# A GLA and RWKV-7 hybrid step on one core: GLA states kept in DRAM between the passes, 28 row buffers, no precedence on TensorE for a pair's products, and transfers that the planner expects later

## Chip, cores and metric

One Trainium2 chip, of which the kernel uses one core. The metric is device time in microseconds (us) of the whole program, one launch; lower is better. TensorE is called PE here, VectorE DVE, ScalarE ACT, GpSimd POOL, and SyncE, which issues the transfers, SP.

## The reference

One layer of a decoder step over a prompt of 1024 tokens and 8 sample tokens, all in float32. Two branches run on the same input: gated linear attention (GLA, 4 heads with a state of 128 x 256) and RWKV-7 (16 heads with a state of 64 x 64, handled as 8 pairs of heads). Both carry a state along the tokens:

```python
p = jnp.einsum('btd,dn->btn', x, w_in)                      # 1024 -> 9360 columns
# GLA:  S_t = diag(a_t) S_{t-1} + k_t^T v_t ;  o_t = q_t S_t
o_gla, S_gla = _gla_chunked(q, k, v, log_a, S_gla0)
# RWKV: S_t = S_{t-1} (diag(w_t) - kk_t^T (kk_t * a_t)) + v_t^T k_t ;  y_t = S_t r_t
y, S_rwkv = _rwkv7_scan(r, w, k, v, kk, a, S_rwkv0)
m = sigmoid(gate_a) * (o_gla @ w_up_gla) + sigmoid(gate_b) * (o_rwkv @ w_up_rwkv)
y_out = _layernorm(DEEPNORM_ALPHA * x + m @ w_out, ln_g, ln_b, LN_EPS)
```

The outputs are `y_out` of both groups and the new states.

## The kernel before

**Passes.** The prompt is cut into two passes: pass 0 has 512 prompt tokens and the 8 sample tokens (matmuls of 260 columns, two per weight block), pass 1 the other 512 (matmuls of 512 columns). Each pass projects all columns of `w_in`, block by block of 128. A weight block and the input are split into a high and a low part (`whi`, `wlo`, `xh`, `xl`), and each product is three matmuls, `proj<-xh,whi`, `proj<-xl,whi` and `proj<-xh,wlo`. Pass 0 writes the split weights to DRAM (`wh`, `wl`), pass 1 reads them back. After both passes come the up-projections of GLA and RWKV for both passes, which load their inputs from DRAM (`o_gla`, `o_rwkv`), and at the end the product with `w_out`.

**What runs beside the projection.** Each of the 8 pairs of a pass is a stream of operations (`pair`): `front` prepares factors and writes the masked products `gg<-big`; SP then copies four blocks of `gg` to DRAM (`LD<-gg`) and reads them back rearranged (`wide<-LD`); DVE solves triangular systems from that in 31 steps (`Xt<-X,wide`, `X<-X,Xt`); and `chain` carries the pair's state over 8 chunks of 64 tokens. One chunk of the chain is a loop through two engines: PE `pch<-wide,gg`, DVE copies it (`rh<-pch`), PE `pch<-rh,XT`, a copy to `wide`, PE `pch<-wide`, and DVE makes the next state (`wide<-pch,pc,s0p`), from which the next chunk starts. The chains of the 16 pairs (8 in each pass) run one after another. Each of the 4 GLA heads is another stream (`gla_head`), and so are the weight splits, the evacuations and the gates.

**What sets the order.** All streams are merged at build time by a planner (`Order.run`) that writes one fixed order for each engine and for SP's queue; on the chip each engine works through its own order, and an instruction whose input is late holds those behind it. The planner takes, of the operations that are next in their streams, the one with the smallest key: its expected start, less a precedence. For operations on PE the precedence is `ON_PE[kind]`, for other engines `PRIO[kind]`, both in us. The expected start adds `HOP[by]` to the time when an input is ready, `by` being the engine that made it, `D` for a transfer:

```python
key = t - (s.on_pe if s.op.eng == "P" else s.prio)
```

A stream names its kind as it goes on: `pair` in `front`, then `turn` (its transposes), `chain` and `norm`; GLA's heads are `head`, the projection `block` with a precedence of 0.

**Buffers.** `SBUF` lists the rotating buffers; `row` is the common one, 128 x 520 float32, of which there are 26. `GS` holds the four GLA states, 128 x 256 each, in SBUF: pass 0 leaves a head's state there and pass 1 starts from it.

Of the kernel before, what the change touches and what calls it, by code (L numbers as in the profile page):

```python
# [10 lines left out]
F32 = mybir.dt.float32  # L11
# [9 lines left out]
P = 128  # L21
D = 1024
# [4 lines left out]
HT = TP // 2  # L27

PASS = [(0, HT + NS, NS, [(0, 260), (260, 260)]), (HT + NS, HT, 0, [(0, 512)])]
GH, GDK, GDV = 4, 128, 256  # L30
# [5 lines left out]
NGC = HT // GC  # L36
# [7 lines left out]

HALF = HT + NS
SBUF = {
    "row": ([P, HALF], 26), "wide": ([P, 2 * HT], 4), "gg": ([P, 4 * HT], 2), "lw": ([P, HT], 2),
    "l2s": ([P, 2 * P], 1), "pc": ([P, NCH], 3), "X": ([P, 256], 1),
    "Xt": ([P, P], 1), "S": ([P, GDV], 2), "s0p": ([P, C], 2), "rh": ([P, P], 2),
    "sto": ([P, P], 1), "Xs": ([P, 3 * P], 1), "bnd": ([P, 1], 3), "st": ([P, 32], 3), "part": ([P, HALF], 2), "l2p": ([P, 2 * P], 2),  # L50
# [10 lines left out]
SPARE_ROWS = 8  # L61


HOP = {"P": 0.2, "D": 0.26, "G": 0.14, "V": 0.14, "A": 0.14}

SWITCH = 0.09
HOLD = 0.11
# [7 lines left out]

PRIO = {"evacuate": 0.7, "pair": 0.4, "turn": 0.5, "chain": 0.5, "norm": 0.1, "x": 0.7, "lora": 0.2, "rank": -0.3,
        "head": 0.3, "gate": 0.05, "w": 0.3, "out": -0.1, "state": 0, "block": 0.0}
ON_PE = {"evacuate": 0.0, "pair": 0.15, "turn": 0.1, "chain": 0.15, "norm": 0.15, "x": 0.0, "lora": 0.15, "rank": 0.1,
         "head": 0.1, "gate": 0.06, "w": 0.0, "out": -0.03, "state": 0.1, "block": 0.0}

URGENT = 0.6
# [62 lines left out]
def price(eng, name, out, args, ins):  # L144
# [3 lines left out]
    if eng == "P":  # L148
# [8 lines left out]
        return 2 * (m + n) / 1200 * rows * cols / P ** 2  # L157
    if eng == "S":
        return 0.48
# [45 lines left out]
class Engine:  # L205
# [3 lines left out]
    def __getattr__(self, name):  # L209
        def make(out, *args, **kw):  # L210
# [3 lines left out]
            for eng, handle in self._handles.items():  # L214
                call = getattr(handle, "tensor_copy" if (eng, name) == ("V", "copy") else name)
                ways.append((eng, lambda call=call: call(out, *args, **kw), price(eng, name, out, args, ins)))  # L216
                if eng in "VG" and shared(eng, name, out, ins):
                    port += eng
            if eng == "S":
                lag = transfer(out, args[0])  # L220
# [8 lines left out]
class Stream:  # L229
# [4 lines left out]
    def be(self, name):  # L234
        self.kind, self.prio, self.on_pe = name, PRIO[name], ON_PE[name]


class Order:
# [4 lines left out]
    def __init__(self, nc):  # L243
        self.P, self.A, self.V, self.G, self.S, self.E, self.C = (Engine(**e) for e in (
            {"P": nc.tensor}, {"A": nc.scalar}, {"V": nc.vector}, {"G": nc.gpsimd}, {"S": nc.sync},
            {"V": nc.vector, "G": nc.gpsimd}, {"A": nc.scalar, "V": nc.vector}))
# [75 lines left out]
    def start(self, op):  # L322

        best = None
        for eng, fn, cost in op.ways:
            free, t = self.time[eng] + (SWITCH if eng == "P" and op.tiles != self.tiles else 0.0), 0.0
            for x in (op.out, *op.ins):
                at, by = self.ready.get(x.tensor.name, (0.0, None))
                if eng == "S" and by == "D" and x is op.out:
                    continue  # L330
                if by != eng:
                    at += HOP.get(by, 0.0) + (SPARE if eng == "P" and by in ("V", "A", "G") else 0.0)
                elif eng != "P" and x is not op.out:
# [70 lines left out]
class Kern(Order):  # L404
# [71 lines left out]
    def setup(self):  # L476
        nc, a = self.nc, self.a
        E = mybir.EngineType
        self.es.enter_context(self.tc.manual_schedule(engines={E.PE, E.Activation, E.DVE, E.Pool, E.SP}))
        cp = self.pool("const")  # L480
        wp = self.pool("w", side="left")
        self.dr = self.pool("dr", space=DRAM)
        pp = self.pool("psum", space=PSUM)
        xp = self.pool("x", side="right")
        self.r1 = r1 = self.pool("work", side="left")
        for tag, bufs in BANKS.items():
            self.buffers(tag, bufs, lambda tag=tag, bufs=bufs: pp.tile([P, 512], F32, name=tag, bufs=bufs))
        for tag, (shape, bufs) in SBUF.items():
            dt = F32R if tag in PARTS else F32
            self.buffers(tag, bufs, lambda tag=tag, shape=shape, bufs=bufs, dt=dt:  # L490
                         r1.tile(shape, dt, name=tag, bufs=bufs))
        for tag, (shape, bufs) in WBUF.items():
            dt = F32 if tag == "wraw" else F32R
            self.buffers(tag, bufs, lambda tag=tag, shape=shape, bufs=bufs, dt=dt:
                         wp.tile(shape, dt, name=tag, bufs=bufs))
        for k in range(NK):
            for v in "hl":
                tag = f"x{v}{k}"
                self.buffers(tag, 1, lambda tag=tag: xp.tile([P, HALF], F32R, name=tag, bufs=1))
        nc.scalar.preload_act_table_set(EXP)  # L500
        self.cons = cp.tile([P, CST_W], F32, name="cons")
        self.pv = cp.tile([P, PV_W], F32, name="pv")
        self.ident = self.cst("ident")
        self.omu = cp.tile([P, NRC], F32, name="omu")
        self.oka = cp.tile([P, 8], F32, name="oka")
        self.nkk = cp.tile([P, 8], F32, name="nkk")
        self.bias = {}
        for n, v in [("glaeps", GLA_EPS), ("gneps", GN_EPS), ("lneps", LN_EPS), ("one", 1.0),
                     ("kkl", 0.5 * math.log(KK_SCALE))]:
            t = cp.tile([P, 1], F32, name="b_" + n)  # L510
            nc.vector.memset(t, v)
            self.bias[n] = t
        dbg = getattr(self, "dbg", {})
        self.o_gla = dbg.get("o_gla", None) or self.dr.tile([D, T], F32, name="o_gla")
        self.o_rwkv = dbg.get("o_rwkv", None) or self.dr.tile([D, T], F32, name="o_rwkv")
        self.sg = [[[self.dr.tile([P, PASS[i][1]], F32, name=f"sg{i}{n}{k}") for k in range(NK)] for n in range(2)]
                   for i in range(2)]
        self.mg = [[self.dr.tile([P, PASS[i][1]], F32, name=f"mg{i}{k}") for k in range(NK)] for i in range(2)]

        self.lev = cp.tile([P, 64 * MASKED], F32, name="lev")  # L520

        self.onesr = cp.tile([P, P], F32R, name="onesr")
        self.headsr = cp.tile([P, P], F32R, name="headsr")
        self.wa = cp.tile([P, NK * 16], F32, name="wa")
        self.alr = [cp.tile([96, HALF], F32R, name=f"alr{n}") for n in range(2)]
        self.gw2 = cp.tile([96, GH * GDK], F32R, name="gw2")
        self.GS = [cp.tile([P, GDV], F32, name=f"GS{h}") for h in range(GH)]

        self.smp = cp.tile([P, 4, NPAIR, NS], F32, name="smp")
        self.RS = self.dr.tile([4, NS, D], F32, name="RS")  # L530
        self.WA = self.dr.tile([2, NS, D], F32, name="WA")
        self.tail = cp.tile([P, NS + 1, NRC], F32, name="tail")
        self.carry = cp.tile([P, NRC], F32, name="carry")
        self.shT = cp.tile([P, NRC, NS], F32, name="shT")
        self.reset = cp.tile([P, HT], U8, name="reset")
        nc.vector.memset(self.reset, 1)
        nc.vector.memset(self.reset[:, ::C], 0)

        self.Sp = [cp.tile([P, C], F32, name=f"Sp{n}") for n in range(NPAIR)]
        for t in self.Sp:  # L540
            nc.gpsimd.memset(t, 0.0)

        for tag, n, bufs in (("az", 4 * HT, 2), ("XT", 2 * HT, 2), ("Lp", HT, 1), ("As", HT, 1)):
            ts = [cp.tile([P, n], F32, name=f"{tag}{i}") for i in range(bufs)]
            for t in ts:
                nc.gpsimd.memset(t, 0.0)
            self.fixed(tag, ts)
# [222 lines left out]
    def gla_head(self, c, h, rows, g):  # L770
        a, n, A, V, E, S_ = self.a, c.n, self.A, self.V, self.E, self.S
# [38 lines left out]
        for lv, m in enumerate(LEVELS):  # L810
            nb = P // (2 * m)
            pl = (yield from self.bank("big", [P, NGC, nb, m])) if lv else None
            wide = lv < MASKED
# [25 lines left out]
            self.free(*([pl] if lv else [r, r2, dd]))  # L839
            tot = nt_  # L840

        S = self.GS[h] if c.i else None

        def vk(x):
            s = slice(x * P, (x + 1) * P)
# [9 lines left out]
        for x in range(NGC):  # L855
            s = slice(x * P, (x + 1) * P)
            VKn = (yield from vk(x + 1)) if x < NGC - 1 else None
            pb = yield from self.bank("big", [P, 4, P])
            po, pS = pb[:, 0:2], pb[:, 2:4].rearrange("p a b -> p (a b)")
            for j in range(2):  # L860
                yield self.P.matmul(po[:, j], VK[:, j * P:(j + 1) * P], AT[:, x], start=True, stop=(S is None))
                if S is not None:
                    yield self.P.matmul(po[:, j], S[:, j * P:(j + 1) * P], qp_[:, s], start=False, stop=True)
            yield self.P.matmul(pS, VK[:, 2 * P:], VK[:, 0:GDV], start=True, stop=True)
            for j in range(2):
                yield A.copy(v[j][:, s], po[:, j])
            Sn = self.GS[h] if x == NGC - 1 else (yield from self.get("S"))
            if S is not None:
                yield V.scalar_tensor_tensor(Sn, S, tot[:, x:x + 1], pS, ALU.mult, ALU.add)
                if x:  # L870
                    self.free(S)
            else:
                yield V.tensor_copy(Sn, pS)
            self.free(pb)
            S, VK = Sn, VKn
        if c.i:
            yield S_.dma_start(self.o["gla_p"][0, 0, h], S)
        else:
            yield from self.gla_sample(h, q, k, v, al, [(AT_, z), (km_, vk1)], qp_)
        s0, s1 = z, vk1  # L880
        self.free(AT_, q, k, al)
# [806 lines left out]
```

## Time and profile before

| | us |
|---|---|
| median of 3 runs | 1630.18 (1628.06 to 1632.21) |
| the profiled execution, its own time | 1629.18 |
| its span, first to last instruction | 1627.4 |
| PE busy | 1579.8 (97%) |
| weight loads of PE (PEld) busy | 1394.6 (86%) |
| DVE busy | 1226.9 (75%) |
| ACT busy | 844.6 (52%) |
| POOL busy | 92.3 (6%) |

Shares are of the span. A matmul's end is modelled, and neighbouring matmuls overlap in the record, so a wait on PE shows only where it is longer than that overlap. The granted TensorE clock was 0.992 over the span. Line numbers say little here, since a helper in line 216 (`make` in `Engine`) records nearly every operation: the names of the tiles tell which is which.

### The profile page before, as it was taken

How to read it: one execution, taken by the hardware profiler on the slowest of the kernel's cores; microseconds unless marked ns; L12 is line 12 of the kernel's file. 1: busy time of each engine (PE TensorE's matmuls, PEld its weight loads, DVE VectorE, ACT ScalarE, POOL GpSimd, SP SyncE). 2: the span in 40 equal slices, each digit the busy share in tenths (PEclk: the TensorE clock that was granted, in tenths of full speed). 3: DMA queues.
4: the chain of work that ended last, by engine and by line, in shares of the span. 5: the costliest groups of instructions: out<-in, count | busy, mean ns of one | idle time of the engine just before them, and what ended most of it. 6: DMA issues, size and time to landing. Idle time of an engine off the chain costs nothing.

```text
span 1627.4 us, 29876 instructions
## 1 busy us (share of the span) xinstructions
PE 1579.8 (97%) x10066; PEld 1394.6 (86%) x10066; DVE 1226.9 (75%) x3201; ACT 844.6 (52%) x2054; POOL 92.3 (6%) x185
## 2 busy tenths in 40 slices
PE   8999999999999999999999999999999999999998
PEld 7899999989999998788877887788788889977786
DVE  6786897788888887678677987898676784666555
ACT  5446765656566656463625472446354555554210
POOL 1100000101010000000100011100000000000000
PEclk9999999999999999999999999999999999999999
DMA  9877785696568765754465546544654487789432
GB/s 291 254 228 235 219 263 174 188 285 207 168 199 284 220 205 173 235 166 131 149 187 156 149 148 208 178 115 150 188 156 132 139 251 226 253 276 289 155 111 84
DMA packets 339572, 318.42 MB, mean 196 GB/s; under 512 B 103011, under 2 KB 225004, under 8 KB 339420
## 3 DMA queue, kind: packets, MB, share of 16 engines
q1 hardware_dynamic: 339420, 316.52, 62.9%
q8 instruction: 80, 1.31, 0.4%
q14 instruction: 72, 0.59, 0.1%
HBM read 197.55 MB, written 117.82 MB: 194 GB/s over the span
## 4 chain that ended last, share of the span: by engine, by line
PE 71%; DVE 12%; DMA 6%; SPq 4%; ACT 3%; issue 2%; POOL 0%; POOLq 0%; DVEq 0%; ACTq 0%
PE proj L216 41%; PE big L216 20%; PE pY L216 6%; SPq L216 4%; PE pch L216 4%; DVE row L216 4%; DVE X L216 2%; DVE wide L216 2%; DVE Xt L216 1%; DMA wide<-LD 1%; ACT row L216 1%; DMA wlo<-wl 1%; DVE wlo L216 1%; DMA row<-xT 1%; DMA row<-o_gla 1%
## 5 line engine op out<-in xcount | busy, mean ns | idle before, releaser
L216 PE MATMUL proj<-xh,whi 128*128 128x260 f32 (+1 forms) x1872 | 617.3, 330 | 3.8 <-DMA whi<-wh 3.1
L216 PE MATMUL proj<-xh,wlo 128*128 128x260 f32 (+1 forms) x1872 | 617.0, 330 | 1.5 <-DMA wlo<-wl 1.0
L216 PE MATMUL proj<-xl,whi 128*128 128x260 f32 (+1 forms) x1872 | 616.7, 329 | 0.0
L216 PEld LDWEIGHTS proj<-xh,whi 128*128 128x128 f32 x1872 | 355.5, 190 | 29.9 <-issue 4.6
L216 PEld LDWEIGHTS proj<-xh,wlo 128*128 128x128 f32 x1872 | 355.3, 190 | 28.7 <-issue 3.0
L216 PEld LDWEIGHTS proj<-xl,whi 128*128 128x128 f32 x1872 | 355.4, 190 | 23.3 <-issue 2.5
L216 ACT CAST whi<-wraw 128x512 fp32r<-128x512 f32 x210 | 130.0, 621 | 100.1 <-PE proj L216 51.5
L216 DVE TENSOR_TENSOR row<-row 128x512 f32<-128x512 f32 (+9 forms) x334 | 164.1, 498 | 11.7 <-ACT row L216 4.2
L216 DVE TENSOR_TENSOR wlo<-wraw,whi 128x512 fp32r<-128x512 f32 x205 | 141.3, 692 | 39.4 <-ACT whi L216 35.8
L216 ACT ACTIVATE row<-row 128x512 f32<-128x512 f32 (+4 forms) x229 | 138.1, 610 | 38.1 <-DVE row L216 28.7
L216 DVE TENSOR_TENSOR Xt<-X,wide 128x60 f32<-128x60 f32 (+24 forms) x496 | 105.1, 212 | 43.2 <-DMA wide<-LD 32.4
L216 ACT ACTIVATE row<-proj,omu 128x260 f32<-128x260 f32 (+1 forms) x99 | 54.3, 548 | 137.9 <-PE proj L216 137.2
L216 PE MATMUL big<-row 128*128 128x64 f32 (+4 forms) x712 | 115.9, 280 | 2.8 <-DVE row L216 1.8
L216 DVE TENSOR_TENSOR X<-X,Xt 128x60 f32<-128x60 f32 (+24 forms) x496 | 105.0, 212 | 12.5
L216 ACT ACTIVATE s0p<-wide,pc 64x64 f32<-64x64 f32 x256 | 87.9, 343 | 41.7 <-DVE wide L216 37.7
L216 PEld LDWEIGHTS big<-row 128*128 128x128 f32 (+1 forms) x712 | 98.1, 192 | 12.5 <-DVE row L216 4.6
L216 ACT COPY wide<-pch 64x64 f32<-64x64 f32 x216 | 44.6, 207 | 97.5 <-PE pch L216 94.2
L216 DVE SCALAR_TENSOR_TENSOR wide<-pch,pc,s0p 64x64 f32<-64x64 f32 x224 | 63.0, 281 | 42.7 <-PE pch L216 38.5
L216 DVE SCALAR_TENSOR_TENSOR row<-proj,pv,row 128x259 f32<-128x259 f32 (+1 forms) x99 | 56.4, 570 | 42.3 <-ACT tail L216 28.7
L216 ACT COPY row<-big 128x128 f32<-128x128 f32 (+7 forms) x161 | 46.0, 309 | 68.0 <-PE big L216 66.7
L216 POOL TENSOR_TENSOR row<-row 128x512 f32<-128x512 f32 (+5 forms) x35 | 38.2, 1092 | 580.7 <-ACT row L216 188.7
L216 PE MATMUL big<-az,wide 128*128 128x256 f32 x256 | 65.9, 382 | 0.3 <-ACT wide L216 0.2
(255 smaller groups left out, 2647.4 us busy)
## 6 DMA issues: line engine op xcount, KB each, us to landing
wraw<-w_in SPq DMA_DIRECT2D x146, 256.0 KB
wh<-whi SPq DMA_DIRECT2D x146, 256.0 KB
wl<-wlo SPq DMA_DIRECT2D x146, 256.0 KB
whi<-wh SPq DMA_DIRECT2D x146, 256.0 KB
wlo<-wl SPq DMA_DIRECT2D x146, 256.0 KB
wide<-LD SPq DMA_DIRECT2D x64, 128.0 KB
wraw<-w_up_gla SPq DMA_DIRECT2D x32, 256.0 KB
wraw<-w_up_rwkv SPq DMA_DIRECT2D x32, 256.0 KB
```

What stands on the lines that cost most here:

```text
L216: ways.append((eng, lambda call=call: call(out, *args, **kw), price(eng, name, out, args, ins)))
```

## The change

Four edits. (1) The GLA states `GS` become DRAM tensors: pass 0 writes a head's last state there, pass 1 reads it into an `S` buffer just ahead of its first use, and the last state always lies in an `S` buffer, of which there are still 2. (2) `row` has 28 buffers instead of 26. (3) `ON_PE` is 0.0 for `pair`, `turn`, `chain` and `norm` (0.15, 0.1, 0.15 and 0.15 before). (4) `HOP["D"]` is 0.8 instead of 0.26.

```diff
-    "row": ([P, HALF], 26), "wide": ([P, 2 * HT], 4), ...
+    "row": ([P, HALF], 28), "wide": ([P, 2 * HT], 4), ...
...
-HOP = {"P": 0.2, "D": 0.26, "G": 0.14, "V": 0.14, "A": 0.14}
+HOP = {"P": 0.2, "D": 0.8, "G": 0.14, "V": 0.14, "A": 0.14}
...
-ON_PE = {"evacuate": 0.0, "pair": 0.15, "turn": 0.1, "chain": 0.15, "norm": 0.15, "x": 0.0, "lora": 0.15, "rank": 0.1,
+ON_PE = {"evacuate": 0.0, "pair": 0.0, "turn": 0.0, "chain": 0.0, "norm": 0.0, "x": 0.0, "lora": 0.15, "rank": 0.1,
...
-        self.GS = [cp.tile([P, GDV], F32, name=f"GS{h}") for h in range(GH)]
+        self.GS = [self.dr.tile([P, GDV], F32, name=f"GS{h}") for h in range(GH)]
...
-        S = self.GS[h] if c.i else None
+        S = None
+        if c.i:
+            S = yield from self.get("S")
+            yield S_.dma_start(S, self.GS[h])
...
-            Sn = self.GS[h] if x == NGC - 1 else (yield from self.get("S"))
+            Sn = yield from self.get("S")
             if S is not None:
                 yield V.scalar_tensor_tensor(Sn, S, tot[:, x:x + 1], pS, ALU.mult, ALU.add)
-                if x:
-                    self.free(S)
+                self.free(S)
...
-        if c.i:
-            yield S_.dma_start(self.o["gla_p"][0, 0, h], S)
-        else:
+        yield S_.dma_start(self.o["gla_p"][0, 0, h] if c.i else self.GS[h], S)
+        self.free(S)
+        if not c.i:
             yield from self.gla_sample(h, q, k, v, al, [(AT_, z), (km_, vk1)], qp_)
```

The same matmuls are issued as before; what moves is their order, and that of the other engines. Three places show how.

DVE, fifth pair of pass 1: from the last masked product `gg` to the first step of the solve, `Xt<-X,wide`, which needs the transfer `wide<-LD`. Before:

```order
L216 TENSOR_TENSOR gg<-big,cons 128x512 x4
L216 TENSOR_REDUCE st<-row 128x8
L216 TENSOR_TENSOR row<-st,row 128x512
L216 TENSOR_TENSOR row<-row 128x512 x2
L216 COPY rh<-pch 128x128
L216 TENSOR_TENSOR row<-row 128x512 x2
L216 TENSOR_REDUCE row<-row 128x8
L216 SCALAR_TENSOR_TENSOR wide<-pch,pc,s0p 64x64 x2
L216 COPY rh<-pch 128x128
L216 TENSOR_TENSOR Xt<-X,wide 128x31
```

The same place now, from the first update of the chain's state on:

```order
L216 SCALAR_TENSOR_TENSOR wide<-pch,pc,s0p 64x64 x2
L216 TENSOR_TENSOR row<-st,row 128x512
L216 TENSOR_TENSOR row<-row 128x512
L216 COPY rh<-pch 128x128
L216 TENSOR_TENSOR row<-row 128x512 x2
L216 COPY wide<-pch 64x64 x2
L216 TENSOR_TENSOR row<-row 128x512
L216 SCALAR_TENSOR_TENSOR wide<-pch,pc,s0p 64x64 x2
L216 TENSOR_REDUCE row<-row 128x8
L216 SCALAR_TENSOR_TENSOR row<-row 128x512
L216 COPY rh<-pch 128x128
L216 TENSOR_TENSOR Xt<-X,wide 128x31
```

A second update of the chain's state, with the copies on both sides of it, has moved ahead of the solve's first step. Over all 16 pairs, 303 DVE instructions now stand between a pair's last `gg` and its first `Xt`, 208 before: more in 12 pairs, as many in 2, fewer in 2 (14 became 9, 10 became 7).

SP, seventh pair of pass 1: the trip through DRAM and the reload of split weights that follows. Before:

```order
L216 DMA LD_15300<-gg 32x8x32 x4
L216 DMA Lp_184<-gg 32x4x32 x4
L216 DMA wide<-LD_15300 32x1024 x4
L216 DMA whi<-wh_0_7966 128x512
L216 DMA wlo<-wl_0_7969 128x512
```

The same place now:

```order
L216 DMA LD_15298<-gg 32x8x32 x4
L216 DMA Lp_184<-gg 32x4x32 x4
L216 DMA whi<-wh_0_7884 128x512
L216 DMA wide<-LD_15298 32x1024 x4
L216 DMA wlo<-wl_0_7918 128x512
```

One weight load has moved between the write of `LD` and its read. Every pair now has some transfer besides `Lp` at that place; before, 5 of 16 had.

PE, fourth chunk of the sixth chain of pass 1: from the chunk's first product to the product that needs DVE's copy `rh`. Before:

```order
L216 MATMUL pch<-wide,gg 128x128
L216 MATMUL pY<-az_177,wide 128x128
L216 MATMUL proj<-xl_9744,whi 128x512
L216 MATMUL proj<-xh_9703,wlo 128x512
L216 MATMUL proj<-xh_9712,whi 128x512
L216 MATMUL pch<-rh,XT_181 128x128
```

The same place now:

```order
L216 MATMUL pch<-wide,gg 128x128
L216 MATMUL pY<-az_177,wide 128x128
L216 MATMUL proj<-xl_9621,whi 128x512
L216 MATMUL proj<-xh_9616,wlo 128x512
L216 MATMUL proj<-xh_9629,whi 128x512
L216 MATMUL proj<-xl_9691,whi 128x512
L216 MATMUL pch<-rh,XT_181 128x128
```

One more matmul of the projection stands between the two. Over the 128 chunks it is 7.5 matmuls on average there, 6.4 before, and 7.7 instead of 6.5 between `pch<-rh,XT` and `pch<-wide`.

More of the change, by code (lines that the diff above doesn't have):

```diff
@@ L46 @@
 SBUF = {
-    "row": ([P, HALF], 26), "wide": ([P, 2 * HT], 4), "gg": ([P, 4 * HT], 2), "lw": ([P, HT], 2),
+    "row": ([P, HALF], 28), "wide": ([P, 2 * HT], 4), "gg": ([P, 4 * HT], 2), "lw": ([P, HT], 2),
     "l2s": ([P, 2 * P], 1), "pc": ([P, NCH], 3), "X": ([P, 256], 1),
```

## The prediction

> **What bounds the kernel now.** I read the shares of busy time first, then the span in three stretches, then PE's waits, and then followed the two largest of them back through the timelines of DVE and SP.
>
> ```profile
> PE 1579.8 (97%) x10066; PEld 1394.6 (86%) x10066; DVE 1226.9 (75%) x3201; ACT 844.6 (52%) x2054; POOL 92.3 (6%) x185
> ```
> ```profile
> 0.00:40.00 40.00, 34.95 (x254) 29.11 (x255) 28.37 (x64) 21.45 (x49) 7.80 (x19) 1.00 0.93 292
> 40.00:1580.00 1540.00, 1505.23 (x9620) 1332.47 (x9620) 1173.25 (x3096) 821.20 (x1998) 81.70 (x163) 0.99 0.64 196
> 1580.00:1627.40 47.40, 39.65 (x195) 33.01 (x194) 25.24 (x42) 1.99 (x8) 2.77 (x3) 0.95 0.26 89
> ```
>
> The columns behind the stretch are the busy time of PE, PEld, DVE, ACT and POOL. PE bounds the kernel, and the change takes no matmul away, so only PE's idle time can be won: 1627.4 - 1579.8 = 47.6 us. Of it 5.0 us lie in the first 40 us and 7.8 us in the last 47, where nothing that the change touches runs; 34.8 us are left between. Who ends those waits is in the list of PE's waits (total, times, longest):
>
> ```profile
> PE big L216 <- DMA row<-xT: 7.1, 3, 4.0
> PE pch L216 <- DVE wide L216: 6.2, 7, 2.0
> PE pch L216 <- DVE rh L216: 4.5, 5, 1.5
> PE big L216 <- DVE part L216: 3.2, 7, 0.9
> PE proj L216 <- DMA whi<-wh: 3.1, 2, 2.5
> PE big L216 <- DVE row L216: 1.8, 3, 0.9
> ...
> PE proj L216 <- DMA wlo<-wl: 1.0, 1, 1.0
> ...
> PE big L216 <- DVE l2p L216: 0.6, 1, 0.6
> ...
> PE proj L216 <- ACT row L216: 0.4, 1, 0.4
> ```
>
> The chain of the pairs (`pch`) has the most, 10.7 us in 12 waits, always for DVE; transfers have 4.1 us at the projection's weights. DVE is only 75% busy, so why is it late? Its own largest wait for a transfer:
>
> ```profile
> DVE Xt L216 <- DMA wide<-LD: 32.4, 13, 4.6
> ...
> DVE l2p L216 <- DMA l2s<-lora: 13.2, 10, 5.8
> ```
>
> In 13 of 16 pairs DVE stands at the first step of the solve, 2.5 us on average, until the trip through DRAM has landed. What that does to PE is seen twice in the timelines, here in the fifth pair of pass 1, first DVE, then PE:
>
> ```profile
> 1049.08 0.29 DVE L216 COPY rh<-pch 128x128 f32<-128x128 f32 x1 [1.01 <-PE pch L216]
> 1052.53 0.19 DVE L216 TENSOR_TENSOR Xt<-X,wide 128x31 f32<-128x31 f32 x1 [3.16 <-DMA wide<-LD]
> ...
> 1054.04 0.59 DVE L216 SCALAR_TENSOR_TENSOR wide<-pch,pc,s0p 64x64 f32<-64x64 f32 x2
> ```
> ```profile
> 1052.36 0.38 PE L216 MATMUL pY<-gg,wide 128*128 128x128 f32 x2
> 1054.78 0.46 PE L216 MATMUL pch<-wide,gg 128*128 128x128 f32 x2 [2.04 <-DVE wide L216]
> ```
>
> The chain's update of `wide` stood in DVE's order behind `Xt`, which waited 3.16 us; PE paid 2.04 us of that. The other, in the sixth chain of pass 1, again DVE, then PE:
>
> ```profile
> 1208.40 0.19 DVE L216 TENSOR_TENSOR Xt<-X,wide 128x31 f32<-128x31 f32 x1 [2.27 <-DMA wide<-LD]
> 1208.62 0.29 DVE L216 COPY rh<-pch 128x128 f32<-128x128 f32 x1
> ```
> ```profile
> 1207.39 0.39 PE L216 MATMUL proj<-xh,wlo 128*128 128x512 f32 x1
> 1207.62 0.40 PE L216 MATMUL proj<-xh,whi 128*128 128x512 f32 x1
> 1208.97 0.49 PE L216 MATMUL pch<-rh,XT 128*128 128x128 f32 x2 [0.95 <-DVE rh L216]
> ```
>
> These rows also give a unit: matmuls of 512 columns start 0.23 us apart, while a record lasts 0.39, so that waits under about 0.16 us do not show as idle.
>
> **The planner's transfers expected later (`HOP`).** It puts more work ahead of whatever needs a transfer. From the order: 303 DVE instructions instead of 208 between a pair's last `gg` and its first `Xt`. At DVE's mean of 1226.9 / 3201 = 0.38 us the 95 more are 36 us, 2.3 us for a pair, against a mean wait of 2.5 us. That would fill the wait, were it spread evenly; it isn't: two pairs get fewer instructions and two as many as before. The sixth chain's wait above belongs to one of the latter, with 6 instructions before and now. I take 60% of the 32.4 us as filled. What PE gets of it: at most all of its 10.7 us of `pch` waits, at least nothing (PE's waits may have other causes, and the solve's later start moves the pair's later steps). PE pays 2.04 of 3.16 us in one example and 0.95 of 2.27 in the other, about half; over the 13 waits it can't have been as much, since 10.7 us are all there is. Half of the 10.7 us is my value: **-5.5 us**. The cover that DVE's fill uses is work that was due anyway; were it gone, the solve would wait again, and PE with it.
>
> The same edit puts a weight load between the write and the read of `LD` on SP, which before went out behind them:
>
> ```profile
> 1198.95 1.80 SPq L216 DMA_DIRECT2D LD<-gg  x4
> ...
> 1203.52 1.86 SPq L216 DMA_DIRECT2D wide<-LD  x4
> 1205.47 0.37 SPq L216 DMA_DIRECT2D whi<-wh  x1
> ```
>
> The read started 2.8 us after the four writes were issued (1198.95 + 1.80), and the `whi` load stood behind it. Now it fills that time. If its buffer is still held by PE, it delays the read instead; the row above that waits for `wide<-LD` would then grow. PE's waits for weights are 3.1 + 1.0 us, and one for `row<-xT` at the change of passes is what 7.1 leaves beside the start, about 2. Ends: -6.1 and, with one more wait as long as the longest, +2.5. I take **-2 us**.
>
> **No precedence for a pair's products (`ON_PE`).** With 0.15 the planner chose a pair's product over a projection matmul that could start up to 0.15 us sooner, so PE was planned to stand; with 0.0 it no longer is. From the order: one matmul more (7.5 for 6.4, 7.7 for 6.5) between a chain's products and the next that depends on them, 0.12 us in pass 0 (half the width) or 0.23 us in pass 1. A wait can lose no more than that. The list has some 25 waits for DVE's products that a pair's PE work shows; at 0.2 us each that is 5 us, beside waits too short to show. The other end is 0 on those rows, or a loss if the longer chain delays something. It can't be the end of the kernel. The last chain's products start at 1410.4:
>
> ```profile
> L216 PE MATMUL pch<-wide x256: 270/273/377, 147.5 to 1410.4; 128*128 128x128 f32 x128
> ```
> ```profile
> 1435.51 5.59 PE pY L216 x24
> ...
> 1608.47 5.55 PE pY L216 x24
> ```
>
> In the order the last chain ends 5844 projection matmuls into the program, 5891 before, and the blocks that need its result begin at 6216. From 1435 us to the end the chain of waits shows groups of 24 matmuls of 512 columns, the first and last of which stand here, in 5.6 us, 0.23 each: the tail streams. I take **-2.5 us**, half of the visible part.
>
> **GLA states through DRAM.** Eight transfers of 128 KB more, 4 writes in pass 0 and 4 reads in pass 1; no engine's work grows. A transfer of that size, issue on SP and first use on DVE:
>
> ```profile
> 1266.09 0.61 SPq L216 DMA_DIRECT2D l2s<-lora  x1
> ```
> ```profile
> 1269.45 0.29 DVE L216 CAST l2p<-l2s 128x256 fp32r<-128x256 f32 x1 [0.39 <-DMA l2s<-lora]
> ```
>
> 3.4 us. A write is waited for only by the same head's read, a pass later; on SP it stands until DVE's last state is made, as the store of the output did in pass 1, with `vd` and weight transfers behind it. Each read stands on SP behind weight loads that wait for a buffer; from the matmul that frees that buffer to the first that reads `S`, PE's order has 25, 35, 34 and 36 matmuls. The 25 are 12 of 512 columns at 0.23 and 13 of 128 columns in full float32 at about 0.22, 5.6 us, more than 3.4 + 0.6; the others have over 7 us. Ends: 0, and 4 x 3.4 = +13.6 us if PE stood for each read in full. I take **0**, since three reads have twice the time needed. [...]
>
> **28 rows.** PE's waits name the release of a bank by ACT's copy to `row` with 0.4 us. Ends -0.4 and 0; I take 0. The two rows enter the order above all.
>
> **The sum.** -5.5 - 2 - 2.5 + 0 + 0 = -10 us on the profiled execution's 1629.2 (span 1627.4 and 1.8 around it): 1619.2. It lies 1.0 below the median of the runs, 1630.2, so that I predict **1619.5**.
>
> **Rivals.** (a) The waits only move. 32.4 us of DVE's waits go, but the solve starts later, other products queue behind it, and PE finds new ones; the fewer instructions in two pairs speak for it, the 12 pairs with more against it. It gives 1629, give or take 5. Chance 0.18. (b) Slower: the reads of `S` are exposed. If SP is held past the point above, a read issued late is waited for by PE directly, in order, with `pb`'s bank held. It decides when SP is more than 5.6 - 4.0 = 1.6 us late for the tightest head and 3.5 for the rest. SP's queue is in fact held by PE and DVE often, which speaks for it; the planner's 0.8 for transfers speaks against. With half of the gains above kept it gives 1629 + 13.6 - 5 = 1638. Chance 0.12, with other losses of that size. (c) A much larger gain. The chain is freed altogether, all 10.7 us, and `part`, `row`, weights, in all 3.2 + 1.8 + 4.1 more, and hidden waits of 5 us: 1629 - 25 = 1604. Chance 0.08. [...]
>
> **How the numbers follow.** The forecast, a gain of 5 to 20 us, has 0.62. The measurement can't tell less than about 0.3%, 4.9 us, from no change. Faster: 0.62 + 0.08 = 0.70; same 0.18; slower 0.12. The range reaches from (c)'s edge, 1606, to 1633, which takes in (a) and leaves out most of (b) and half of (c): under 2 in 10.
>
> **What would show it.** DVE's row for `Xt` waiting for `wide<-LD` falls from 32.4 us to 10 to 20, in fewer pairs; PE's two `pch` rows from 10.7 to about 5; PE's idle time from 47.6 to 37 or 38. A row of PE waiting for `S<-GS` over 2 us makes the GLA term wrong; `whi` or `wlo` rows over 5 us the term of SP. The prediction is wrong if the row of `Xt` falls and the time doesn't.

## The result and the profile after

The changed kernel takes 1607.01 us (median of 4 runs, 1605.45 to 1607.85); the kernel before, run beside it, 1629.12 (4 runs, 1621.84 to 1632.21). The ratio is 0.987, with a 95% interval of 0.9835 to 0.9904. The profiled execution took 1607.75 us, 21.4 less than that of before. First the shares of busy time, then the span in three stretches (us; busy time of PE, PEld, DVE, ACT, POOL; granted clock, DMA share, GB/s):

```profile
PE 1568.2 (98%) x10066; PEld 1394.8 (87%) x10066; DVE 1225.4 (76%) x3206; ACT 835.5 (52%) x2046; POOL 91.7 (6%) x184
```
```profile
0.00:40.00 40.00, 34.33 (x250) 28.79 (x251) 28.57 (x64) 21.23 (x48) 7.80 (x19) 1.00 0.90 288
40.00:1559.00 1519.00, 1494.65 (x9628) 1333.29 (x9627) 1171.68 (x3102) 812.30 (x1990) 81.09 (x162) 0.99 0.65 200
1559.00:1606.00 47.00, 39.21 (x193) 32.68 (x191) 25.10 (x41) 1.99 (x8) 2.77 (x3) 0.96 0.27 90
```

The gain has two parts. PE's idle time fell from 47.6 to 1606.0 - 1568.2 = 37.8 us, all of it in the middle stretch (34.8 to 24.4). And PE's busy time fell by 11.6 us with the same 10066 matmuls. I read this as waits shorter than the overlap of two records, which a profile counts as busy (0.16 us between two matmuls of 512 columns, which start 0.23 us apart with records of 0.39); what supports that reading is measured further below. PE's waits (total, times, longest), and DVE's two rows for transfers:

```profile
PE big L216 <- DMA row<-xT: 5.7, 2, 4.0
PE big L216 <- DVE Sp L216: 5.5, 2, 2.9
PE pch L216 <- DVE wide L216: 2.7, 5, 1.1
PE pch L216 <- DVE rh L216: 2.3, 4, 1.0
PE big L216 <- ACT part L216: 2.1, 1, 2.1
PE big L216 <- DMA S<-GS: 1.7, 2, 1.0
...
PE proj L216 <- DMA wlo<-wl: 0.5, 1, 0.5
...
PE big L216 <- DVE part L216: 0.4, 1, 0.4
```
```profile
DVE Xt L216 <- DMA wide<-LD: 18.6, 10, 3.6
...
DVE l2p L216 <- DMA l2s<-lora: 4.2, 4, 1.4
```

The chain's two rows have halved (10.7 to 5.0), the weights' are nearly gone (4.1 to 0.5). One wait is new: 5.5 us for `Sp`, the state at a chain's end that PE transposes. It is the old mechanism at another place. First DVE, then PE, at 1135 us in pass 1:

```profile
1134.92 0.19 DVE L216 TENSOR_TENSOR Xt<-X,wide 128x31 f32<-128x31 f32 x1 [3.60 <-DMA wide<-LD]
...
1137.67 0.59 DVE L216 SCALAR_TENSOR_TENSOR Sp<-pch,pc,s0p 64x64 f32<-64x64 f32 x2
```
```profile
1138.32 0.42 PE L216 MATMUL big<-cons,Sp 128*64 128x128 f32 x1 [2.95 <-DVE Sp L216]
```

`Sp` stood in DVE's order behind the first four steps of the next pair's solve, eight instructions. The first of them stood 3.60 us for `LD`, and the eight then took 2.75 us; PE's wait of 2.95 us began 0.4 us after DVE's had ended. And PE paid once more. The same core in three stretches of 3.3 us: during the wait, just after it, and after that:

```profile
1134.70:1138.00 3.30, 0.67 (x3) 0.19 (x1) 2.74 (x10) 0.91 (x2) 1.26 (x1) 1.00 1.04 386
1138.30:1141.60 3.30, 3.29 (x9) 2.61 (x10) 2.70 (x11) 1.00 (x3) 0.00 (x0) 0.51 0.31 94
1141.80:1145.10 3.30, 3.30 (x15) 2.66 (x15) 2.85 (x14) 0.00 (x0) 0.00 (x0) 1.00 0.26 88
```

After the wait the granted clock was 0.51, and 9 matmuls started where 14 start at 1.00 (the counts in the rows take in those still running at a row's start), though PE reads as fully busy in both. Matmuls of 512 columns started 0.43 us apart in it and 0.23 us apart after it. Such a stretch at half clock costs about half its length, an estimate: 0.47 of it by this spacing, 0.49 by the clock, 0.36 by the counts. Before and after the change have four of them, 20.5 us in all in either, so that they don't explain the 11.6 us of busy time.

### The profile page after: what moved, and what is told of

Read it like the earlier page. It is cut to its first block, busy times and chain, and to the rows that moved or that the text cites. A ratio compares the mean times of both kernels' runs of the same rounds, so it can differ in the third digit from the quotient of the medians.

```text
span 1606.0 us, 29861 instructions
## 1 busy us (share of the span) xinstructions
PE 1568.2 (98%) x10066; PEld 1394.8 (87%) x10066; DVE 1225.4 (76%) x3206; ACT 835.5 (52%) x2046; POOL 91.7 (6%) x184
## 4 chain that ended last, share of the span: by engine, by line
PE 84%; DVE 6%; DMA 4%; ACT 2%; issue 2%; SPq 1%; POOL 0%; POOLq 0%; DVEq 0%; ACTq 0%
PE proj L216 49%; PE big L216 22%; PE pY L216 8%; PE pch L216 5%; DVE row L216 2%; SPq L216 1%; DMA wide<-LD 1%; DVE wide L216 1%; DVE Xt L216 1%; ACT row L216 1%; DVE X L216 1%; DMA wlo<-wl 1%; DMA S<-GS 1%; DVE az L216 0%; ACT wide L216 0%
## 5 line engine op out<-in xcount | busy, mean ns | idle before, releaser
L216 PEld LDWEIGHTS proj<-xh,whi 128*128 128x128 f32 x1880 | 356.5, 190 | 25.8 <-issue 1.7
L216 DVE TENSOR_TENSOR row<-row 128x256 f32<-128x256 f32 (+10 forms) x327 | 162.1, 499 | 16.4 <-ACT row L216 6.8
L216 ACT ACTIVATE row<-row 128x512 f32<-128x512 f32 (+5 forms) x229 | 138.4, 611 | 34.7 <-DVE row L216 24.2
L216 DVE TENSOR_TENSOR Xt<-X,wide 128x60 f32<-128x60 f32 (+24 forms) x496 | 108.3, 218 | 30.4 <-DMA wide<-LD 18.6
L216 DVE TENSOR_TENSOR X<-X,Xt 128x60 f32<-128x60 f32 (+24 forms) x496 | 105.0, 212 | 11.6
L216 PEld LDWEIGHTS big<-row 128*128 128x128 f32 (+1 forms) x712 | 94.2, 190 | 9.9 <-DVE row L216 2.3
L216 POOL TENSOR_TENSOR row<-row 128x512 f32<-128x512 f32 (+3 forms) x42 | 47.5, 1137 | 663.2 <-DVE row L216 223.7
```

## The experiments

Each ratio is to the kernel before, run beside it on the same chip, with its 95% interval. The experiments were measured in three groups, in which the median of before was 1624.2, 1622.8 and 1624.3 us (23, 17 and 11 runs). `HOLD`, a cost that the planner adds in another choice and that no part of the change touches, served to make neutral reorderings: the same work and settings, another order, and for a few operations another engine (DVE has 3188 instructions instead of 3201 in the first).

**Transfers expected later, alone** (on the kernel before):

```diff
-HOP = {"P": 0.2, "D": 0.26, ...
+HOP = {"P": 0.2, "D": 0.8, ...
```

> The kernel before with the planner's hop for transfers at 0.8 alone. Mechanism theory (the hop fills DVE's wait for the trip through DRAM): DVE's row of Xt waiting for wide<-LD falls from 32.4 us to under 22, PE's two pch rows from 10.7 to under 7, time 8 to 14 us under before. Precedence theory (the hidden short waits are the larger half, and they go with ON_PE): row of Xt falls all the same, time only 3 to 7 us under before. Reshuffling theory (any new order moves the time by some us, whichever edit makes it): no tie between the row of Xt and the time; anything from -12 to +8 us.

Measured: 1630.31 us, 1.0047 (1.0028 to 1.0066), slower by 0.5%: of the three ranges that were set for it only that of reshuffling holds it. PE's waits and DVE's row:

```profile
PE pch L216 <- DVE wide L216: 6.7, 7, 2.3
...
PE big L216 <- DVE Xs L216: 6.1, 2, 4.1
PE pch L216 <- DVE rh L216: 5.8, 10, 1.4
PE proj L216 <- DMA wlo<-wl: 3.0, 1, 3.0
```
```profile
DVE Xt L216 <- DMA wide<-LD: 19.5, 10, 4.8
```

DVE's wait for `LD` fell as in the whole change, from 32.4 to 19.5 us, but PE's chain waits didn't (12.5 us, 10.7 before), and 6.1 us of waits for `Xs`, the solve's result that PE needs next, came. The row of `Xt` alone doesn't carry the time.

**No precedence, alone** (on the kernel before):

```diff
-ON_PE = {..., "pair": 0.15, "turn": 0.1, "chain": 0.15, "norm": 0.15, ...
+ON_PE = {..., "pair": 0.0, "turn": 0.0, "chain": 0.0, "norm": 0.0, ...
```

> The kernel before with ON_PE at 0.0 for pair, turn, chain and norm alone. Mechanism theory: row of Xt stays near 32 us, hidden waits fall, time 4 to 9 us under before. Precedence theory: 12 to 18 us under before, with PE's busy time lower by 8 or more. Reshuffling theory: anything from -12 to +8 us.

Measured: 1631.82 us, 1.0044 (1.002 to 1.0067), slower by 0.4%, again inside the range of reshuffling alone. Its profile shows 44.4 us at half clock, the most of all. Three stretches of it, about one of its two waits for `Xs`:

```profile
280.00:290.00 10.00, 6.45 (x54) 6.27 (x52) 5.15 (x13) 7.84 (x14) 0.00 (x0) 0.99 0.67 167
290.70:300.90 10.20, 8.91 (x43) 8.59 (x43) 4.21 (x9) 5.43 (x13) 0.12 (x1) 0.54 0.99 331
301.00:311.00 10.00, 9.87 (x79) 9.32 (x78) 6.38 (x13) 9.25 (x19) 1.98 (x6) 1.00 0.36 112
```

After 3.6 us of waiting in the first stretch (busy 6.45 of 10) the clock stayed at half for 10.2 us: 43 matmuls, then 79. The hidden waits did shrink here (`work` in the table below), but the half clock and the long waits used that up.

**GLA states in DRAM and 28 rows, alone** (on the kernel before):

```diff
-    "row": ([P, HALF], 26), ...
+    "row": ([P, HALF], 28), ...
-        self.GS = [cp.tile(...) for h in range(GH)]
+        self.GS = [self.dr.tile(...) for h in range(GH)]
...
```

> The kernel before with the GLA states in DRAM and 28 rows alone, hop and ON_PE as before. Mechanism and precedence theories: within 3 us of before, since no wait of PE names a row. Rival, that the two rows matter after all by letting fronts start earlier: 5 to 10 us under before. Reshuffling theory: anything from -12 to +8 us.

Measured: 1641.16 us, 1.0114 (1.0088 to 1.014), outside every range that was set for it. Its reads of `S` cost PE 3.1 us, not the 17 lost; its large waits stand elsewhere, 6.1 us for `Xs` and 4.7 for `xh` in the up-projections. Taken alone this reads as a loss by the edit; the next run shows that it needn't be one.

**A neutral reordering of before:**

```diff
-HOLD = 0.11
+HOLD = 0.12
```

> The kernel before with the planner's cost HOLD at 0.12 instead of 0.11, an edit that has no purpose but to give a new order (nearly every row of PE's order moves). Mechanism and precedence theories: within 4 us of before. Reshuffling theory: 5 us or more from before, to either side, as much as a single edit of the change.

Measured: 1646.37 us, 1.0144 (1.0117 to 1.0171): slower than any edit, with no setting of the change touched. One place where it lost, PE's wait, then DVE ahead of it, then three stretches:

```profile
373.42 0.85 PE L216 MATMUL big<-Xs,Lp 128*128 128x32 f32 x3 [6.20 <-DVE Xs L216]
```
```profile
367.05 1.38 DVE L216 TENSOR_TENSOR az<-row 64x512 f32<-64x512 f32 x2
368.44 0.17 DVE L216 COPY pc<-row 128x8 f32<-128x8 f32 x1
368.52 2.58 DVE L216 TENSOR_TENSOR wide<-row 64x512 f32<-64x512 f32 x4
371.12 1.42 DVE L216 SCALAR_TENSOR_TENSOR row<-row,pv 128x512 f32<-128x512 f32 x2
372.46 0.68 DVE L216 TENSOR_TENSOR wlo<-wraw,whi 128x512 fp32r<-128x512 f32 x1
373.06 0.30 DVE L216 STREAM_TRANSPOSE Xs<-Xs 128x128 f32<-128x128 f32 x1
```
```profile
364.00:372.00 8.00, 3.21 (x27) 3.01 (x26) 7.91 (x14) 2.51 (x5) 0.78 (x4) 1.00 0.58 150
372.90:383.00 10.10, 9.05 (x29) 7.46 (x30) 5.51 (x11) 2.90 (x8) 0.00 (x0) 0.53 0.73 256
383.00:391.00 8.00, 8.00 (x63) 7.55 (x62) 4.86 (x8) 4.72 (x14) 0.00 (x0) 1.00 0.16 25
```

DVE wasn't waiting: it worked off the next pair's `front` and a weight split (`wlo`), which the order put ahead of `Xs`; PE stood 6.2 us and then ran about 9 us at half clock. One order has this collision and its neighbour hasn't, and that moves the time by more than the edits above. So the three single edits above can't be read as effects of what they edit.

**A second one**, `HOLD` at 0.10 on the kernel before:

```diff
-HOLD = 0.11
+HOLD = 0.10
```

> The kernel before with HOLD at 0.10, another order of the old planner settings. Joint theory with scatter (orders of one setting scatter by some 10 us around a level that hop and ON_PE set; the kernel before is a good draw of a level near 1636): 5 to 25 us over before, PE's pch rows 10 to 14 us. Reshuffling theory without levels: as likely under before as over it.

Measured: 1647.83 us, 1.0142 (1.0122 to 1.0163). With the two runs ahead of it that makes three orders with the old `HOP` and `ON_PE`, 1.011 to 1.014 of the kernel before: as far as four orders can tell, the kernel before is a good draw of its settings, by about 1%.

**Both numbers, without the DRAM trip and the rows** (whole change, `GS` and `row` as before):

```diff
-    "row": ([P, HALF], 28), ...
+    "row": ([P, HALF], 26), ...
-        self.GS = [self.dr.tile(...) for h in range(GH)]
+        self.GS = [cp.tile(...) for h in range(GH)]
...
```

> Hop and ON_PE of the change together, with the GLA states in SBUF and 26 rows as before. After the single edits each came out slower, two theories are left. Joint theory (the two edits of the planner win only together, since the hop puts work ahead of late transfers and ON_PE gives PE the projection to run meanwhile): 15 to 25 us under before, as the whole change. Reshuffling theory (each order is a draw, spread over some 30 us, and the change is a good draw): anything from -10 to +20 us, most likely 5 to 10 us over before.

Measured: 1603.19 us, 0.9864 (0.9831 to 0.9897), as the whole change, 0.987. Its shares:

```profile
PE 1562.8 (98%) x10066; PEld 1392.2 (87%) x10066; DVE 1229.0 (77%) x3181; ACT 845.5 (53%) x2068; POOL 95.2 (6%) x189
```

Busy time and idle time (1601.1 - 1562.8 = 38.3 us) are both as low as in the whole change. The trip through DRAM and the two rows neither give nor take more than orders differ by anyway.

**The whole change with the old `HOP`:**

```diff
-HOP = {"P": 0.2, "D": 0.8, ...
+HOP = {"P": 0.2, "D": 0.26, ...
```

> The whole change, with the hop back at 0.26. Joint theory: the gain is gone, 0 to 10 us over before, and DVE's row of Xt waiting for wide<-LD back over 25 us. Reshuffling theory: anything from -10 to +20 us, whatever that row does.

Measured: 1620.80 us, 0.9985 (0.9961 to 1.0009). Shares, and one row of PE's waits:

```profile
PE 1568.7 (97%) x10066; PEld 1394.0 (86%) x10066; DVE 1231.6 (76%) x3198; ACT 838.3 (52%) x2047; POOL 100.1 (6%) x195
```
```profile
PE proj L216 <- DMA whi<-wh: 3.5, 2, 2.2
```

Busy time is as low as in the whole change; idle is back, 1615.0 - 1568.7 = 46.3 us, with the wait for weights that the later expectation had removed. DVE's row of `Xt` is 14.3 us here, less than in the whole change, where over 25 was expected, and the time is that of before.

**The whole change with the old `ON_PE`:**

```diff
-ON_PE = {..., "pair": 0.0, "turn": 0.0, "chain": 0.0, "norm": 0.0, ...
+ON_PE = {..., "pair": 0.15, "turn": 0.1, "chain": 0.15, "norm": 0.15, ...
```

> The whole change, with ON_PE back at 0.15, 0.1, 0.15, 0.15. Joint theory: the gain is gone, 0 to 10 us over before, row of Xt under 22 us. Reshuffling theory: anything from -10 to +20 us.

Measured: 1641.60 us, 1.010 (1.0057 to 1.0144), over the 0 to 10 us of the joint theory. Busy time (1577.7 us) and idle time (62.7) are those of the orders with the old settings again; the largest wait is a single one for `xh`, split from a reload (`o_gla`) at the up-projections:

```profile
PE pY L216 <- ACT xh L216: 8.2, 1, 8.2
PE pch L216 <- DVE wide L216: 7.9, 8, 1.9
```

**Neutral reorderings of the whole change**, `HOLD` at 0.12 and at 0.10:

```diff
-HOLD = 0.11
+HOLD = 0.12
```

> The whole change, with the planner's cost HOLD at 0.12 instead of 0.11, for another order and nothing else. Joint theory: within 6 us of the whole change, 15 us or more under before. Reshuffling theory: the gain is mostly gone, 10 us or more over the whole change, as the same edit cost the kernel before 23 us.

```diff
-HOLD = 0.11
+HOLD = 0.10
```

> The whole change with HOLD at 0.10, another order of the new settings. Joint theory with scatter: 15 to 35 us under before, PE's pch rows under 8 us, PE waiting for DVE's Xs under 2 us. Reshuffling theory without levels: anything from -30 to +20 us.

Measured: 1592.86 us, 0.981 (0.9779 to 0.9841) at 0.12, the fastest of all and better than both kernels (its interval just touches that of the whole change; by the ratios it is 10 us under it, where the joint theory had at most 6); 1607.43, 0.9893 (0.9876 to 0.9911) at 0.10. So the gain of the two numbers holds in four orders out of four (these two, the whole change, and the one without the DRAM trip), and they lie 0.8% apart. Their mean is 0.986; that of the four orders with the old numbers is 1.010, so that by these eight, an estimate, the two numbers are worth about 2.4%. In the one at 0.10 DVE stands 25.8 us at `Xt`, the chain's rows are 9.5 us and that for `Xs` 2.7, the last two more than expected, and it is as fast as the whole change.

**A later expectation still**, whole change:

```diff
-HOP = {"P": 0.2, "D": 0.8, ...
+HOP = {"P": 0.2, "D": 1.4, ...
```

> The whole change with the hop for transfers at 1.4 instead of 0.8. If the planner's transfers are still expected too early (18.6 us of DVE's waits for wide<-LD are left): that row under 10 us, and 0 to 8 us under the whole change. If 0.8 is past what PE can use: that row falls all the same, time within 5 us of the whole change or over it.

Measured: 1607.78 us, 0.989 (0.9872 to 0.9908). `Xt` falls to 11.1 us and the chain's waits to 4.3, and nothing is gained by it, as the second expectation had it: idle is 39.0 us.

**Precedence taken from the chain only**, whole change, `pair`, `turn` and `norm` as before:

```diff
-ON_PE = {..., "pair": 0.0, "turn": 0.0, "chain": 0.0, "norm": 0.0, ...
+ON_PE = {..., "pair": 0.15, "turn": 0.1, "chain": 0.0, "norm": 0.15, ...
```

> The whole change, but of the four ON_PE entries only chain at 0.0; pair 0.15, turn 0.1 and norm 0.15 as before. If the chain's precedence is what costs (its pch waits): 12 us or more under before, pch rows under 8 us. If the precedence of the solve's products (turn, pair) is what costs, through PE parked at big<-Xs,Lp: not under before by more than 8 us, and that row at 5 us or more.

Measured: 1618.88 us, 0.9961 (0.9946 to 0.9976). Neither expectation came whole: the gain is small, and yet PE's row for `Xs` is only 1.0 us. The chain's waits are as low as in the whole change, 3.2 + 1.5 us, but others come:

```profile
PE proj L216 <- ACT row L216: 5.6, 2, 4.8
PE pY L216 <- ACT xh L216: 4.6, 1, 4.6
PE proj L216 <- DMA wlo<-wl: 3.9, 2, 3.4
```

**All runs together.** Idle is the span less PE's busy time. Half is the time at half clock between the first 5 and the last 12 us, added up from the records of the granted clock. "Work" is PE's busy time less half of that, an estimate of what is left of busy at full clock. `Xt` is DVE's wait for `wide<-LD`, `pch` PE's two rows, `w` PE's rows for `whi<-wh` and `wlo<-wl`. All in us but the ratio. The columns from idle on come from one execution each, which took from 4.1 us less than the median of its run (0.26, 0 with DRAM) to 6.6 us more (chain 0).

| `HOP` D, `ON_PE` | run | ratio | idle | half | work | Xt | pch | w |
|---|---|---|---|---|---|---|---|---|
| 0.26, old | before | 1 | 47.6 | 20.5 | 1569.6 | 32.4 | 10.7 | 4.1 |
| | HOLD 0.12 | 1.0144 | 67.1 | 30.7 | 1563.1 | 33.2 | 11.8 | 2.9 |
| | HOLD 0.10 | 1.0142 | 63.6 | 23.9 | 1570.1 | 28.0 | 12.4 | 3.9 |
| | DRAM, 28 rows | 1.0114 | 59.3 | 30.7 | 1564.5 | 29.5 | 11.9 | 2.5 |
| 0.8, old | alone | 1.0047 | 53.2 | 30.7 | 1565.2 | 19.5 | 12.5 | 3.6 |
| | DRAM, 28 rows | 1.0100 | 62.7 | 27.3 | 1564.0 | 22.8 | 12.6 | 2.1 |
| 0.26, 0 | alone | 1.0044 | 52.7 | 44.4 | 1558.1 | 22.1 | 10.7 | 2.5 |
| | DRAM, 28 rows | 0.9985 | 46.3 | 20.5 | 1558.5 | 14.3 | 6.1 | 3.5 |
| 0.8, chain 0 | DRAM, 28 rows | 0.9961 | 48.9 | 37.5 | 1555.9 | 14.6 | 4.7 | 4.2 |
| 0.8, 0 | without DRAM, 26 rows | 0.9864 | 38.3 | 13.7 | 1556.0 | 14.9 | 6.4 | 0.2 |
| | whole change | 0.987 | 37.8 | 20.5 | 1558.0 | 18.6 | 5.0 | 0.5 |
| | HOLD 0.12 | 0.981 | 34.4 | 10.2 | 1556.5 | 17.5 | 5.0 | 0 |
| | HOLD 0.10 | 0.9893 | 38.9 | 13.7 | 1557.6 | 25.8 | 9.5 | 0.4 |
| 1.4, 0 | DRAM, 28 rows | 0.989 | 39.0 | 27.3 | 1554.5 | 11.1 | 4.3 | 0 |

Two columns separate without overlap. Work is 1563 to 1570 with the old `ON_PE` and 1554 to 1559 with the chain's at 0, whatever `HOP` is: means of 1566.1 and 1556.9, 9 us apart. Idle is 34 to 39 only where both numbers are changed in full, and 46 to 67 in all nine others. `Xt` alone separates nothing. Part of the idle time has a place: PE's waits for `Xs` are 6.1 to 7.8 us in five of the nine others, and 0.4 to 2.7 in the other nine runs of the table.

## Why the prediction was right, and where not

The time, 1607.0 us, lies in the range of 1606 to 1633, near its low end; the sign was right and the size was not: 22 us (21.4 between the profiled executions) for a forecast of 10, outside the "gain of 5 to 20" and 3 us from rival (c)'s 1604. The sum took the planner's two edits as if each worked alone, which the runs speak against: alone they measured 0.5 and 0.4% over this kernel before, together 1.3% under. That the time still fell into the range, 1.0 us above its end, is in part luck.

- **`ON_PE`, forecast -2.5 us: the term that was mis-sized.** The step took half of "the visible part", 5 us, and set the "waits too short to show" at nothing. These were the larger part: busy time fell by 11.6 us, and the table gives the edit 9 us. I added up how much later each matmul starts after the one ahead of it than the quickest tenth of matmuls with the same pair of shapes, at full clock and without the waits that the records show. This excess separates the six orders with the old values from the other eight, by about 10 us between the means (153 to 161 us against 144 to 150, taken against one quickest tenth for all runs; an estimate, whose level hangs on how that tenth is taken). About 5 of the 10 us stand ahead of the chain's products, the rest mainly before the projection's matmuls and `big<-part`. In the one run that takes the chain's precedence alone, work is 1555.9 us, so that all of the 9 us are there.
- **`HOP`, forecast -5.5 us for the chain.** In the whole change the numbers came as forecast: `Xt` 18.6 us (10 to 20), the chain's rows 5.0 (about 5), idle 37.8 (37 to 38). The cause given, that PE pays about half of what DVE stands at `Xt`, is not what the runs show. Alone the edit cut `Xt` by 13 us and the chain's waits by nothing (12.5), and the time rose by 0.5%. The text's own condition, that "the row of `Xt` falls and the time doesn't", came true in four runs: both with the new `HOP` and the old `ON_PE`, both the other way about. What failed in this term is the link: a shorter stand of DVE was to shorten PE's waits by itself. With `ON_PE` at 0 the edit is worth 1.2 and 1.8% (0.9985 to 0.987 with the DRAM trip, 1.0044 to 0.9864 without).
- **SP's weight load, forecast -2 us.** 3.6 us went, and the row is at most 0.5 in all five runs with both numbers and 2.1 to 4.2 in all others. The later expectation is needed for it and isn't enough. Whether the `whi` load in the gap between `LD`'s write and read does it, as the step has it, no run isolates.
- **GLA states through DRAM, 28 rows, forecast 0.** Borne out within what orders differ by: 0.987 with, 0.9864 without; PE waits 1.7 us for `S<-GS`, under the 2 that was set. That is two of the four reads, though three were said to have twice the time needed, and in three other runs with the trip the row is 2.2 to 3.1 us, over the 2.
- **Rival (a), the waits only move, 0.18.** In part: 5.5 us now stand at `Sp`, behind the same parked solve. It is what the single edits do, that of `HOP` above all. **Rival (b), slower by exposed reads of `S`:** no run shows it. **Rival (c), 1604:** the time nearly, but not its way: the chain kept 5.0 of 10.7 us, what went at `part`, `row` and the weights was in part replaced by 5.5 us at `Sp`, and the hidden waits gave 11.6 us, not 5.

Not foreseen at all: that single orders of one setting lie 0.5 to 1.4% apart, and that half-clock stretches are part of it.

What stays open is why the two numbers win only together. The five runs with both and the nine others show that they do for idle time. With two runs in each of the single cells, 0.5 and 0.6% apart, the joint excess over the sum of both edits in the time, about 1.3%, is likely and no more. My reading, which no run isolates: a product of the pair that stands in PE's order too early waits whether DVE is parked or only busy, and one that is given room still waits when DVE is parked.

## What to carry to other kernels

Where a planner fixes the order, a neutral change of its constants measures what any reordering is worth; here that was up to 1.4%, so an edit of the order is judged by several orders with it and without it, and the settings of two numbers together, not each alone. When a bound engine is 97% busy, ask how many of its instructions follow a dependency closely: waits shorter than the records' overlap (0.16 us here between matmuls of 512 columns) read as busy, and by the reading above they were half of this gain. If one wait is removed from the list, look at what stood behind the same parked instruction.

## What the runs showed of the hardware

A wait on PE of a few us cost more than itself here. Between the first 8 and the last 12 us of the 14 profiles, 28 of the 29 waits over 2.3 us had a stretch at a granted clock of 0.5 beside them (running at the wait's end or begun within 3.6 us of it), and 27 of the 77 waits of 1.2 to 2.3 us; the stretches lasted 3.4, 6.8 or 10.2 us and took 10 to 44 us of a run, so they cost an estimated 5 to 22 us. In the 3.4 us ahead of a stretch PE stood 0.8 to 3.4 us in all, some of it in several short waits. The 2.5 us wait of the kernel before that ends at 996.5 us has one too, from 997.7 to 1001.1 us, so that the first row takes in its larger part:

```profile
998.60:1002.00 3.40, 3.40 (x11) 2.69 (x10) 2.92 (x15) 0.00 (x0) 0.00 (x0) 0.62 1.04 395
1002.00:1005.40 3.40, 3.40 (x16) 2.72 (x16) 0.91 (x3) 0.74 (x2) 1.36 (x2) 1.00 0.76 239
```

The length of a wait alone doesn't decide it. Waits of 1.2 to 2.9 us had a stretch beside them in many places, as one of 1.37 us in the changed kernel did, ending at 1013.6 us, with a stretch from 1015.5 us. One of 1.80 us in the kernel before, ending at 888.4 us, had none (granted clock 1.00 from 888.4 to 892.0 us), and neither had one of 2.33 us (`HOP` alone, ending at 895.5 us). What else decides, no run isolates.
